# First projections of a two-layer trunk: x loaded with features as rows, scaled after the products

## The chip, the cores and the metric

The kernel runs on one core of one Trainium2 chip. The time is device time in microseconds, the median of three runs; the profile is one more execution, recorded by the hardware profiler. PE (TensorE) multiplies matrices, DVE (VectorE), ACT (ScalarE) and POOL (GpSimd) work elementwise, SP (SyncE) and ACT issue DMA transfers. PSUM is the memory that PE writes its products into, in eight banks here of 128 x 512 floats.

## The reference

The input x has 512 rows (tokens) of 1024 features, in float32. Two layers follow one another; only the start of the first is touched here:

```python
h = rms_norm(x, ev_pre_g)                 # x * rsqrt(mean(x*x) + 1e-6) * g, by row
c_q, c_kv, k_rope, dq, dk, dv = split_cols(h @ w_in, (256, 128, 32, 512, 512, 512))
q = heads_first(rms_norm(c_q, cq_g) @ w_uq, 8)        # latent attention (MLA)
kv = heads_first(rms_norm(c_kv, ckv_g) @ w_ukv, 8)
o_mla = mla_attention(q_nope, q_rope, k_nope, rope(k_rope, pos), v_mla)
o_diff = diff_attention(...)              # on dq, dk, dv: softmax 1 - lambda * softmax 2
x = x + rms_norm(concat(o_mla, o_diff) @ w_out, ev_post_g)
x = x + rms_norm(conv_ffn(rms_norm(x, ffn_pre_g), ...), ffn_post_g)
```

The row factor rsqrt(mean(x*x) + eps) can be taken out of a product with w_in, since it belongs to a row of x and the product sums over features; the weight g cannot, since it belongs to a feature. Where a second norm follows (c_q, c_kv), the row factor cancels but for eps: the norm of the unscaled product with eps * (mean(x*x) + eps) in place of eps is the same number. The second layer (dilated and stick-breaking attention) and its FFN follow in the same manner and are not touched.

## The kernel before, in words

Every float32 product is made of three products of a shorter format: `mm3` multiplies the high half by the high half, high by low and low by high. So every operand is split: ACT rounds it to its high half (`wh`, `xh`), DVE subtracts to get the low half (`wl`, `xl`). For weights the class `Weights` does this: `load` issues one DMA on SP's queue into one of three raw buffers `wraw`, `split` makes the halves in one of five pairs of buffers, `next` hands out a pair and keeps `depth` units ahead. A raw buffer comes free when its low half is made, and SP issues its transfers in order.

The opening, in `trunk` and `even`, goes as follows. SP loads X3, the last 128 tokens of x, then the norm weights, the identity for transposes, the four units of `ev_w_c` (416 columns of w_in, two feature blocks of 128 in a unit) and the other tiles X2, X1, X0. Meanwhile PE multiplies zeros (`warm`, 16 products). For each tile in the order 3, 2, 1, 0, `normalise` takes the square sum on ACT (`mean_square`), the power on POOL (`rstd`), scales X by row and by weight on DVE into `xn`, and `turned` transposes `xn` in eight blocks of 128 x 128 on PE; `split` then makes `xh` and `xl`, with features as rows. Products follow: for each tile 24 products of 416 columns into a bank `ac`, then the norms of c_q and c_kv by square sums of `ac` and the rotary part `ra`, all into `ctok`, four transposes into `tc`, and the split into `omh`/`oml`. Then `diff_qk` makes dq and dk of head 0 (48 products `aqk` of 512 columns), and 72 products `auq`, `auk`, `auv` make the queries `mq`, keys `mk` and values `mv` of the latent attention. `tables` loads the masks and slopes on ACT's queue and computes lambda. All this is put in order by the framework's scheduler.

The attention loop after it is written out by hand (`manual_schedule`): for each of 32 units a score product `sps`, a softmax on DVE and ACT, transposes `tpp`, and between them `Fill`, which hands out single products of `diff_v` (values of the differential attention) and of `diff_qk` for heads 1 to 3, so that PE has work while it waits. dq leaves PSUM through ACT with its scale, dk through DVE, dv through both by turns. PSUM banks have tags: three `a`, two `s`, and one each of `t`, `o`, `n`.

The host function `layout` only cuts and permutes the arrays.

Of the kernel before, what the change touches and what calls it, by code (L numbers as in the profile page):

```python
# [9 lines left out]
F32 = mybir.dt.float32  # L10
# [7 lines left out]
P = 128  # L18
S = 512
# [9 lines left out]
WARM = 16  # L29
# [57 lines left out]
def trunk(tc, A, out):  # L87
# [3 lines left out]
    with ExitStack() as top:  # L91
# [39 lines left out]
        load_x(3)  # L131

# [14 lines left out]
        units += [(A["ev_w_c"][u], 832) for u in range(4)]  # L147
# [26 lines left out]
        def rstd(ms, more=None):  # L174
# [3 lines left out]
            POOL.tensor_tensor(v[:, :n], ms, epst[:, :n], ALU.add)  # L178
# [5 lines left out]
        def mean_square(src):  # L184
# [4 lines left out]
            return rstd(ms[:])  # L189
# [383 lines left out]
        def even():  # L573
            with ExitStack() as es:
# [6 lines left out]
                g_pre = gain("ev_pre_g", 0)  # L581
                nc.sync.dma_start(ident[:], A["ident"])
                for n, i in enumerate(ORDER[1:]):
                    W.load()
                    load_x(i)
# [24 lines left out]
                def diff_qk(h, z):  # L610
# [5 lines left out]
                    if z == 0:  # L616
                        ACT.activation(dq[h], acc, AF.Copy, scale=-0.125)
                    else:
                        DVE.tensor_copy(dk[h], acc)

                def diff_v(tiles):
# [9 lines left out]
                    DVE.tensor_copy(dv[:, tiles[0]], accs[0])  # L631
                    ACT.copy(dv[:, tiles[1]], accs[1])
# [34 lines left out]
                def tables():  # L667
# [8 lines left out]
                    nc.scalar.dma_start(lamb, A["ev_lam"].partition_broadcast(P))  # L676
                    v = chp.tile([P, 8], F32, tag="lam", name="lam", bufs=1)
# [42 lines left out]
                with ExitStack() as e1:  # L720
# [4 lines left out]
                    for n, i in enumerate(ORDER):  # L725
                        normalise(i, g_pre, xnT, "tn" if i % 2 else "ss")()
                        W.ahead((2, 3, 4, 4)[n])

                    with ExitStack() as e2:
# [5 lines left out]
                        wc = [W.next() for _ in range(4)]  # L735
                        nc.sync.dma_start(cgain[:, :256], A["ev_cq_g"][0:1, :].partition_broadcast(P))
                        nc.sync.dma_start(cgain[:, 256:], A["ev_ckv_g"][0:1, :].partition_broadcast(P))
                        nc.sync.dma_start(rtab[:], A["rope_tok"])
                        nc.sync.dma_start(qtab[:], A["rope_q"])
                        for i in ORDER:  # L740
                            t = slice(i * P, (i + 1) * P)
                            a = bank("a", "ac")
# [20 lines left out]
                            for k in range(4):  # L763
                                PE.transpose(tp[:, k], ctok[:, k], ident[:])
# [752 lines left out]
```

## Time and profile before

| what | us |
|---|---|
| median of three runs | 1161.83 (1159.96 to 1161.96) |
| the profiled execution | 1159.68 |
| its span | 1157.9 |
| PE, DVE, ACT, POOL busy | 1139.7, 813.0, 555.1, 61.8 |
| first warm-up product | 1.05 |
| first transposes of x | 8.10 |
| first product of the projections | 11.22 |
| first score product of the attention loop | 62.89 |

The span runs from the first to the last instruction of the profiled execution. Line numbers (L263) are lines of the kernel; a helper's line stands for all who call it, so `L263` to `L265` are the three products of `mm3`. PE is counted as busy from the start of a product to its modelled end, and products overlap; their cadence is read from start to start. The granted clock of PE is 0.998 on average.

### The profile page before, as it was taken

The numbers are of one execution on the slowest core, as the hardware profiler recorded it, in microseconds if no ns is written. First come the engines' busy times: TensorE is split into PE (matmuls) and PEld (weight loads), VectorE is DVE, ScalarE is ACT, GpSimd is POOL, SyncE is SP. The second block draws the span as 40 slices with busy tenths as digits, with TensorE's granted clock in tenths as the row PEclk, the third lists the DMA queues.
The fourth block names the chain that finished last, engine by engine and source line by source line (L and its number), as shares of the span: only waits on it lengthen the run. The fifth ranks groups of instructions, "written<-read, shape, count | busy, mean of one in ns | idle before, by whom it ended". The sixth has DMA issues, their size and how long they took to land.

```text
span 1157.9 us, 15198 instructions
## 1 busy us (share of the span) xinstructions
PE 1139.7 (98%) x5668; PEld 936.2 (81%) x5668; DVE 813.0 (70%) x1431; ACT 555.1 (48%) x940; POOL 61.8 (5%) x139
## 2 busy tenths in 40 slices
PE   8999999999999999999999999999999999999997
PEld 7876677898888888888778877888988888888886
DVE  6676677558667667899873565576676766779897
ACT  5555555345444434456543454554443443445562
POOL 2100022210000000000020000002000000000002
PEclk9999999999999999999999999999999999999999
DMA  8410122243332332355634212222232323324461
GB/s 304 149 55 1 55 92 68 79 149 110 95 106 91 92 109 73 109 159 170 226 119 150 73 61 94 90 67 94 93 110 96 105 91 95 105 82 138 146 207 74
DMA packets 39195, 126.82 MB, mean 110 GB/s; under 512 B 4689, under 2 KB 6353, under 8 KB 39121
## 3 DMA queue, kind: packets, MB, share of 16 engines
q1 hardware_dynamic: 37056, 122.11, 32.5%
q10 hardware_dynamic: 2064, 3.74, 1.0%
q8 instruction: 45, 0.74, 0.3%
q14 instruction: 30, 0.24, 0.1%
HBM read 117.95 MB, written 6.29 MB: 107 GB/s over the span
## 4 chain that ended last, share of the span: by engine, by line
PE 45%; issue 2%; DVE 1%; POOL 1%; ACT 1%; POOLq 0%; DVEq 0%; ACTq 0%
PE u L264 7%; PE u L265 7%; PE u L263 7%; PE acc L263 3%; PE acc L264 3%; PE acc L265 3%; PE apt L263 3%; PE apt L264 3%; PE apt L265 3%; PE cp L1182 1%; PE apv L263 1%; PE apv L265 1%; PE apv L264 1%; PE o L1266 1%; PE o L1343 1%
## 5 line engine op out<-in xcount | busy, mean ns | idle before, releaser
L73 DVE TENSOR_TENSOR wl<-wraw,wh 128x1024 fp32r<-128x1024 f32 (+1 forms) x189 | 228.8, 1218 | 179.0 <-ACT wh L72 178.6
L72 ACT CAST wh<-wraw 128x1024 fp32r<-128x1024 f32 (+1 forms) x189 | 195.8, 1046 | 273.1 <-PE u L264 179.7
L264 PE MATMUL u<-xl,wh 128*128 128x512 f32 (+1 forms) x768 | 285.3, 372 | 0.1
L265 PE MATMUL u<-xh,wl 128*128 128x512 f32 (+1 forms) x768 | 285.2, 372 | 0.0
L263 PE MATMUL u<-xh,wh 128*128 128x512 f32 (+1 forms) x768 | 284.9, 372 | 0.1
L264 PEld LDWEIGHTS u<-xl,wh 128*128 128x128 f32 x768 | 144.6, 188 | 25.4 <-DVE xl L172 0.3
L265 PEld LDWEIGHTS u<-xh,wl 128*128 128x128 f32 x768 | 144.6, 188 | 25.1
L263 PEld LDWEIGHTS u<-xh,wh 128*128 128x128 f32 x768 | 144.4, 188 | 25.2 <-ACT xh L171 0.6
L264 PE MATMUL acc<-wl,gh 128*128 128x512 f32 (+1 forms) x250 | 96.9, 387 | 0.0
L265 PE MATMUL acc<-wh,gl 128*128 128x512 f32 (+1 forms) x250 | 96.9, 387 | 0.0
L263 PE MATMUL acc<-wh,gh 128*128 128x512 f32 (+1 forms) x250 | 96.8, 388 | 0.0
L417 ACT ACTIVATE y<-y 128x512 f32<-128x512 f32 x44 | 27.7, 632 | 84.9 <-DVE y L415 84.9
L412 ACT ACTIVATE y<-u,cw 128x512 f32<-128x512 f32 x88 | 67.2, 771 | 1.8 <-PE u L265 1.8
L415 DVE SCALAR_TENSOR_TENSOR y<-u,cw,y 128x510 f32<-128x510 f32 x88 | 65.6, 747 | 2.5
L413 DVE SCALAR_TENSOR_TENSOR y<-u,cw,y 128x511 f32<-128x511 f32 x88 | 65.1, 744 | 0.9 <-ACT y L412 0.9
L178 POOL TENSOR_TENSOR rv<-ms,epst 128x1 f32<-128x1 f32 x39 | 10.9, 283 | 921.7 <-ACT junk L230 843.5
L263 PEld LDWEIGHTS acc<-wh,gh 128*128 128x128 f32 x250 | 46.9, 188 | 10.2 <-issue 0.5
L596 ACT ACTIVATE s<-s,st 128x128 f32<-128x128 f32 (+3 forms) x64 | 35.8, 560 | 40.1 <-DVE st L594 23.2
L265 PEld LDWEIGHTS acc<-wh,gl 128*128 128x128 f32 x250 | 46.9, 188 | 9.6
L264 PEld LDWEIGHTS acc<-wl,gh 128*128 128x128 f32 x250 | 47.0, 188 | 9.5
L263 PE MATMUL apt<-xh,wh 128*128 128x512 f32 x128 | 50.6, 396 | 0.0
L264 PE MATMUL apt<-xl,wh 128*128 128x512 f32 x128 | 50.0, 391 | 0.0
(315 smaller groups left out, 1956.9 us busy)
## 6 DMA issues: line engine op xcount, KB each, us to landing
wraw<-in_ffn_w_up SPq DMA_DIRECT2D x88, 512.0 KB, 3.6
wraw<-in_ffn_w_down SPq DMA_DIRECT2D x44, 512.0 KB, 3.7
wraw<-in_od_w_dqk SPq DMA_DIRECT2D x12, 512.0 KB, 3.6
wraw<-in_ffn_w_down SPq DMA_DIRECT2D x22, 256.0 KB, 2.7
wraw<-in_ev_w_dqk SPq DMA_DIRECT2D x8, 512.0 KB, 3.7
wraw<-in_ev_w_out SPq DMA_DIRECT2D x8, 512.0 KB, 3.4
spill<-X SPq DMA_DIRECT2D x8, 512.0 KB, 2.6
X<-spill SPq DMA_DIRECT2D x8, 512.0 KB, 6.7
```

The lines of the kernel that those rows point to most:

```text
L72: self.nc.scalar.copy(h[:, :w], raw[:, :w])
L73: self.nc.vector.tensor_tensor(l[:, :w], raw[:, :w], h[:, :w].bitcast(F32), ALU.subtract)
L263: PE.matmul(o, lh, rh, start=first, stop=False, skip_group_check=more)
L264: PE.matmul(o, lh, rl, start=False, stop=False, skip_group_check=more)
L265: PE.matmul(o, ll, rh, start=False, stop=last, skip_group_check=more)
L412: ACT.activation(y[:, z], u, AF.Identity, bias=c[:, 3:4], scale=c[:, 2:3])
L413: DVE.scalar_tensor_tensor(y[:, z, 1:], u[:, :S - 1], c[:, 1:2], y[:, z, 1:], ALU.mult, ALU.add)
L415: DVE.scalar_tensor_tensor(y[:, z, 2:], u[:, :S - 2], c[:, 0:1], y[:, z, 2:], ALU.mult, ALU.add)
L417: ACT.activation(y[:, 0], y[:, 0], AF.Silu)
L596: ACT.activation(s[:, :n], s[:, :n], AF.Exp, bias=st[:, 0:1], scale=-1.0, accum_out=st[:, 1:2])
L1182: PE.matmul(zp[:, c + (j2 - j) * P:c + n], tri[:, 0 if j2 == j else 1], part[:, off[j2]:off[j2 + 1]], start=(j2 == j and part is sh), stop ...
L1266: PE.matmul(o12[hp][:, y, r], pt[:, y, rr, g], cv12[:, r, c:c + 64], start=(g == 0), stop=(g == 1))
```

## The change

The host hands over x a second time, with features as rows (`xT`, eight blocks of 128 features by 512 tokens), and the norm weight as columns (`ev_pre_gT`). The blocks are loaded into the buffers `mq`, which are free until the queries are made. `begin_c` rounds xT times the norm weight to `xh` and takes `xl` as the rest, one feature block k at a time, and splits that block's 416 columns of w_c. Nothing is normalised or transposed ahead of the products: x is multiplied without its row factor. The products run for all four tiles together over the first five blocks (`SPREAD`), in four banks, then tile by tile for the last three (`last_c`).

The row factor is made beside them: `square_x` takes the square sums of the tiles X, which are loaded after xT, and POOL makes `rx[0]` (the factor) and `rx[1]` (eps times mean square plus eps). It is put in where products leave PSUM: the norms of c_q and c_kv take `rx[1]` as their eps, the rotary part takes `rx[0]` as a factor, dv is scaled by it on its way out (by DVE and ACT), and dq and dk, whose columns are tokens, are multiplied by `rbc`, the same factor as a row for all partitions. `rbc` comes from four products of a matrix of ones with diagonal matrices and stays in one of the two buffers `gain`. dq now leaves PSUM through DVE in place of ACT.

The stretch is written out by hand under `manual_schedule`, with the transposes of `ctok` and the casts of dq's and dk's weights between the products. `ident`, `rtab` and `cgain` are loaded on ACT's queue in place of SP's. The lambda computation moves from `tables` into a function `lambdas`, called at the fifth unit of the attention loop. The warm-up has 10 products in place of 16.

The diff, each piece moved to the left margin:

```diff
-WARM = 16
+WARM = 10
+SPREAD = 5
...
-load_x(3)
...
-units += [(A["ev_w_c"][u], 832) for u in range(4)]
...
-def rstd(ms, more=None):
+def rstd(ms, more=None, eps=epst):
...
-POOL.tensor_tensor(v[:, :n], ms, epst[:, :n], ALU.add)
+POOL.tensor_tensor(v[:, :n], ms, eps[:, :n], ALU.add)
...
-def mean_square(src):
+def mean_square(src, eps=epst):
...
-return rstd(ms[:])
+return rstd(ms[:], None, eps)
...
-g_pre = gain("ev_pre_g", 0)
-nc.sync.dma_start(ident[:], A["ident"])
-for n, i in enumerate(ORDER[1:]):
-    W.load()
-    load_x(i)
+rx = lead[:, 16:28].rearrange("p (a b) -> p a b", a=3)
+rbc = glob.tile([P, D], F32, tag="gain", name="rbc", bufs=2)[:, :S]
...
-ACT.activation(dq[h], acc, AF.Copy, scale=-0.125)
+DVE.scalar_tensor_tensor(dq[h], acc, -0.125, rbc, ALU.mult, ALU.mult)
...
-DVE.tensor_copy(dk[h], acc)
+DVE.tensor_tensor(dk[h], acc, rbc, ALU.mult)
...
-DVE.tensor_copy(dv[:, tiles[0]], accs[0])
-ACT.copy(dv[:, tiles[1]], accs[1])
+DVE.tensor_scalar(dv[:, tiles[0]], accs[0], rx[:, 0, tiles[0]:tiles[0] + 1], None, ALU.mult)
+ACT.activation(dv[:, tiles[1]], accs[1], AF.Copy, scale=rx[:, 0, tiles[1]:tiles[1] + 1])
...
+    return g, lamb, lj
+def lambdas(g, lamb, lj):
...
-for n, i in enumerate(ORDER):
-    normalise(i, g_pre, xnT, "tn" if i % 2 else "ss")()
-    W.ahead((2, 3, 4, 4)[n])
+gcol = lead[:, 8:16]
+nc.scalar.dma_start(gcol, A["ev_pre_gT"])
+raws, wc, acs = {}, [], [bank(tag, "ac") for tag in "aaao"]
+def fetch(k):
+    nc.sync.dma_start(mq[k][:], A["xT"][k])
+    if k % 2 == 0:
+        raws[k // 2] = wpool.tile([P, 1024], F32, tag="wraw", name="wraw", bufs=3)
+    c = slice((k % 2) * 416, (k % 2 + 1) * 416)
+    (nc.scalar if k == 0 else nc.sync).dma_start(raws[k // 2][:, c], A["ev_w_c"][k // 2, :, c])
+def begin_c(k):
+    if k % 2 == 0:
+        wc.append(W.pair())
+    h, l = wc[k // 2]
+    c = slice((k % 2) * 416, (k % 2 + 1) * 416)
+    raw = raws[k // 2][:, c]
+    ACT.activation(xh[:, k], mq[k][:], AF.Copy, scale=gcol[:, k:k + 1])
+    ACT.copy(h[:, c], raw)
+    DVE.scalar_tensor_tensor(xl[:, k], mq[k][:], gcol[:, k:k + 1], xh[:, k].bitcast(F32),
+                             ALU.mult, ALU.subtract)
+    DVE.tensor_tensor(l[:, c], raw, h[:, c].bitcast(F32), ALU.subtract)
+def product_c(i, k):
+    t = slice(i * P, (i + 1) * P)
+    h, l = wc[k // 2]
+    c = slice((k % 2) * 416, (k % 2 + 1) * 416)
+    mm3(acs[3 - i][:, :416], xh[:, k, t], xl[:, k, t], h[:, c], l[:, c], k == 0, k == KD - 1)
+def square_x(i):
+    junk = chp.tile([P, D], BF16, tag="junk", name="junk", bufs=1)
+    r = [rx[:, n, i:i + 1] for n in range(3)]
+    ACT.activation(junk[:], X[i][:], AF.Square, scale=D ** -0.5, accum_out=r[2])
+    POOL.tensor_tensor(r[1], r[2], epst[:, :1], ALU.add)
+    POOL.tensor_tensor(r[0], r[1], mhalf[:, :1], ALU.pow)
+    POOL.tensor_tensor(r[1], r[1], epst[:, :1], ALU.mult)
...
-wc = [W.next() for _ in range(4)]
-nc.sync.dma_start(cgain[:, :256], A["ev_cq_g"][0:1, :].partition_broadcast(P))
-nc.sync.dma_start(cgain[:, 256:], A["ev_ckv_g"][0:1, :].partition_broadcast(P))
-nc.sync.dma_start(rtab[:], A["rope_tok"])
-nc.sync.dma_start(qtab[:], A["rope_q"])
-for i in ORDER:
-    t = slice(i * P, (i + 1) * P)
-    a = bank("a", "ac")
-    for k in range(KD):
-        wh, wl = wc[k // 2]
-        c = slice((k % 2) * 416, (k % 2 + 1) * 416)
-        mm3(a[:, :416], xh[:, k, t], xl[:, k, t], wh[:, c], wl[:, c], k == 0, k == KD - 1)
-    rq = mean_square(a[:, 0:256])
-    rk = mean_square(a[:, 256:384])
+ctoks = {}
+def squares_c(i):
+    a = acs[3 - i]
+    e = rx[:, 1, i:i + 1]
+    ctoks[i] = mean_square(a[:, 0:256], e), mean_square(a[:, 256:384], e)
+def norm_c(i):
+    a = acs[3 - i]
+    rq, rk = ctoks[i]
+    r = rx[:, 0, i:i + 1]
...
-DVE.tensor_tensor(ra[:, 0], a[:, 384:416], rtab[:, i, 0], ALU.mult)
-DVE.tensor_tensor(ra[:, 1, 0:16], a[:, 400:416], rtab[:, i, 1, 0:16], ALU.mult)
-DVE.tensor_tensor(ra[:, 1, 16:32], a[:, 384:400], rtab[:, i, 1, 16:32], ALU.mult)
+for o, c, z, d in ((ra[:, 0], 384, 0, 0), (ra[:, 1, 0:16], 400, 1, 0),
+                   (ra[:, 1, 16:32], 384, 1, 16)):
+    n = o.shape[1]
+    DVE.scalar_tensor_tensor(o, a[:, c:c + n], r, rtab[:, i, z, d:d + n],
+                             ALU.mult, ALU.mult)
...
+    ctoks[i] = ctok
+def turn_c(i):
...
-    PE.transpose(tp[:, k], ctok[:, k], ident[:])
+    PE.transpose(tp[:, k], ctoks[i][:, k], ident[:])
+t = slice(i * P, (i + 1) * P)
...
-for z in range(2):
-    Fill(diff_qk(0, z)).end()
-tables()
+W.depth = 1
+ones = dv[:, 2, :P]
+POOL.memset(ones, 1.0)
+for k in range(KD):
+    fetch(k)
+for i in ORDER:
+    load_x(i)
+for _ in range(2):
+    W.load()
+nc.sync.dma_start(qtab[:], A["rope_q"])
+W.load()
+with tc.manual_schedule(engines=everything):
+    for k in range(KD):
+        begin_c(k)
+        if k == 1:
+            nc.scalar.dma_start(ident[:], A["ident"])
+            nc.scalar.dma_start(rtab[:], A["rope_tok"])
+        if k == 3:
+            nc.scalar.dma_start(cgain[:, :256], A["ev_cq_g"][0:1, :].partition_broadcast(P))
+            nc.scalar.dma_start(cgain[:, 256:], A["ev_ckv_g"][0:1, :].partition_broadcast(P))
+        if k < SPREAD:
+            for i in ORDER:
+                product_c(i, k)
+    square_x(3)
+    square_x(2)
+    def last_c(i):
+        for k in range(SPREAD, KD):
+            product_c(i, k)
+    last_c(3)
+    squares_c(3)
+    square_x(1)
+    norm_c(3)
+    last_c(2)
+    squares_c(2)
+    square_x(0)
+    norm_c(2)
+    last_c(1)
+    begun = cast(W)
+    squares_c(1)
+    rest(*begun)
+    turn_c(3)
+    last_c(0)
+    norm_c(1)
+    squares_c(0)
+    turn_c(2)
+    dq0, dk0 = [Fill(diff_qk(0, z)) for z in range(2)]
+    dq0(8)
+    norm_c(0)
+    begun = cast(W)
+    dq0(4)
+    turn_c(1)
+    rest(*begun)
+    dq0(6)
+    turn_c(0)
+    dq0(5)
+    dk0(12)
+    rows = bank("s", "rows", NT, P)
+    for i in ORDER:
+        d = dv[:, 3, i * P:(i + 1) * P]
+        DVE.tensor_scalar(d, ident[:], rx[:, 0, i:i + 1], None, ALU.mult)
+        PE.matmul(rows[:, i], ones, d, start=True, stop=True)
+    ACT.copy(rbc, rows.rearrange("p a b -> p (a b)"))
+    dk0(11)
+    dq0.end()
+    dk0.end()
+W.depth = 5
+small = tables()
...
-assert len(W.made) == 13
-made = {9: 14, 27: 15, 30: 16}
+assert len(W.made) == 9
+made = {9: 10, 27: 11, 30: 12}
...
+if n == 4:
+    lambdas(*small)
...
-r = {"x": a["x"][0]}
+r = {"x": a["x"][0], "xT": a["x"][0].T.reshape(KD, P, S), "ev_pre_gT": a["ev_pre_g"][0].reshape(KD, P).T}
```

## The prediction, made before the run

> **What bounds the kernel now.** I read the page first, then busy time by stage.
>
> ```profile
> span 1157.9 us, 15198 instructions
> ...
> 0.00:62.89 62.89, 59.00 (x297) 51.35 (x297) 39.31 (x79) 35.27 (x70) 10.67 (x32) 1.00 0.58 208
> ...
> 62.89:165.00 102.11, 101.60 (x517) 69.85 (x515) 71.69 (x252) 54.28 (x158) 6.50 (x12) 1.00 0.15 47
> ```
>
> A row of stages gives start:end, length, then busy time of PE, weight loads, DVE, ACT and POOL, clock, DMA share, GB/s. The attention stage from 62.89 us has PE busy 101.6 of 102.1 us. The opening loses 3.9 us outright, and fills more with warm-up products. So the opening was read next, in order of time.
>
> ```profile
> 0.74 0.38 SPq L129 DMA_DIRECT2D X<-in_x  x1
> ...
> 1.05 6.64 PE L137 MATMUL warm<-zero 128*128 128x128 f32 x32 [1.05 <-DVE zero L134]
> ...
> 5.14 1.06 ACT L188 ACTIVATE junk<-X 128x1024 bf16<-128x1024 f32 x1 [2.67 <-DMA X<-in_x]
> ...
> 11.22 0.46 PE L263 MATMUL ac<-wh,xh 128*128 128x416 f32 x1 [1.80 <-ACT xh L171]
> ...
> 13.04 0.46 PE L265 MATMUL ac<-wh,xl 128*128 128x416 f32 x1
> ...
> 62.89 0.61 PE L807 MATMUL sps<-mk,mq 128*128 128x128 f32 x4
> ...
> PE ac L263 <- ACT xh L171: 1.8, 1, 1.8
> ...
> PE sps L807 <- DVE st L594: 0.5, 1, 0.5
> ```
>
> A row gives start, length, engine, line, output and inputs. The first product of the projections starts at 11.22 us: ahead of it stand X3's load (landed 5.14), its square sum, the normalisation, the transposes and the split. Its third partner waits until 13.04. The last two rows are from the list of waits: PE waits 1.8 us for the first `xh`, and once 0.5 us later on in the first 110 us. So what bounds the kernel is TensorE's queue of products behind a late start, and a microsecond off the opening is a microsecond off the end if the attention stage still begins without a new wait.
>
> **The change part by part.** The cadence of PE's work, from neighbouring starts:
>
> ```profile
> 15.25 0.35 PE L264 MATMUL ac<-wl,xh 128*128 128x416 f32 x1
> ...
> 15.44 0.60 PE L211 MATMUL tp<-ident,xn 128*128 128x128 f32 x4
> ...
> 15.79 0.43 PE L265 MATMUL ac<-wh,xl 128*128 128x416 f32 x1
> ...
> 17.20 0.35 PE L265 MATMUL ac<-wh,xl 128*128 128x416 f32 x1
> ...
> 17.39 0.35 PE L263 MATMUL ac<-wh,xh 128*128 128x416 f32 x1
> ...
> 39.76 0.39 PE L604 MATMUL aqk<-xh,wh 128*128 128x512 f32 x1
> ...
> 39.99 0.39 PE L606 MATMUL aqk<-xl,wh 128*128 128x512 f32 x1
> ...
> 63.25 0.48 PE L604 MATMUL av<-wh,xh 128*128 128x512 f32 x1
> ```
>
> A 416-column product costs 0.19 us (17.20 to 17.39), a 512-column one 0.227 (39.76 to 39.99). Four transposes between two products make 0.54 us of 0.19 (15.25 to 15.79), so 0.35, and with the longer next one 0.4. A plain 128x128 product costs 0.18 (62.89 to 63.25 holds two).
>
> Before, check of the method: start 11.22, 96 products of 0.19 (18.2), 48 for dq0/dk0 and 72 for auq/auk/auv of 0.227 (27.2), six groups of x transposes and four of c (10 x 0.4 = 4.0) give 60.6; the other 2.3 us to 62.89 are the early waits. After: the eight x groups are gone, four `rows` products come (0.7), so PE has 18.2 + 27.2 + 1.6 + 0.7 = 47.7 us of work behind its start.
>
> *The start.* Now it hangs on k = 0: 256 KB of xT and 208 KB of w_c.
>
> ```profile
> wraw<-in_ffn_w_down SPq DMA_DIRECT2D x22, 256.0 KB, 2.7
> ...
> wraw<-in_ffn_w_down SPq DMA_DIRECT2D x44, 512.0 KB, 3.7
> ...
> 10.00:11.00 1.00, 0.00 (x0) 0.00 (x0) 0.23 (x1) 1.00 (x3) 0.19 (x1) 1.00 1.03 421
> ...
> L201 DVE SCALAR_TENSOR_TENSOR xn<-X,rr,gain 128x512 f32<-128x512 f32 x8 | 5.8, 747 | 7.7 <-POOL rr L181 7.7
> ...
> L73 DVE TENSOR_TENSOR wl<-wraw,wh 128x832 fp32r<-128x832 f32 x4 | 4.1, 1019 | 0.5 <-ACT wh L72 0.5
> ...
> L73 DVE TENSOR_TENSOR wl<-wraw,wh 128x1024 fp32r<-128x1024 f32 x1 | 1.2, 1219 | 0.0
> ...
> L72 ACT CAST wh<-wraw 128x832 fp32r<-128x832 f32 x4 | 3.5, 887 | 2.0 <-DMA wraw<-in_ev_w_c 2.0
> ...
> L72 ACT CAST wh<-wraw 128x1024 fp32r<-128x1024 f32 x1 | 1.1, 1059 | 0.0
> ...
> 1.19 1.28 ACT L188 ACT_TABLE_LOAD   x1 [1.19 <-PEq L1509]
> ```
>
> The rows are DMA issues (us to landing last), a window (GB/s last), groups (mean ns of one before the second bar). A load of 256 KB alone lands 2.7 us after its issue, so 3.4; X3 with twice the bytes landed 4.4 after its own, at 5.14. I take 4.4 us, since alibi, the gain column and the next tiles fly beside it. The activation table load (1.28) now stands behind the gain column's landing and ends by then if that lands by 3.1. From the 832 and 1024 widths a cast is 0.83 ns and a subtraction 1.04 ns a column: ACT 0.63 for 512, 0.54 for 416; DVE 0.59 for 416, and 0.75 for the scaled `xl` (L201's kind). The second product needs `wl`: 4.4 + 0.63 + 0.75 + 0.59 = 6.4 us, my effective start (bounds: 5.4 with the lone load, 7.2 with X3's landing).
>
> *Feeding k = 1 to 7.* PE needs 12 x 0.19 = 2.3 us for a k of all four tiles; ACT 1.2, DVE 1.35, and 0.47 MB at 421 GB/s 1.1 us. So SPREAD = 5 rows cover the loads, and the four DMA issues (`ident`, `rtab`, two `cgain`) that move into ACT's order there, 0.38 us each like X3's on SP; each also waits for an earlier landing, of alibi, xT or `ident`, which comes before the next xT tile that ACT would wait for anyway. The eight normalisations (0.75 each) and the eight splits of transposes that go free DVE and ACT for this. Work ends without a stall at 6.4 + 47.7 = 54.1.
>
> *The waits that come.* ACT now squares X three to four tiles deep among the square sums of `ac`.
>
> ```profile
> L188 ACT ACTIVATE junk<-X 128x1024 bf16<-128x1024 f32 x3 | 3.2, 1059 | 0.4 <-DMA X<-in_x 0.4
> ...
> 24.60 0.38 ACT L188 ACTIVATE junk<-ac 128x256 bf16<-128x256 f32 x1 [0.55 <-PE ac L265]
> ...
> 25.41 0.56 POOL L181 TENSOR_TENSOR rr<-rv,mhalf 128x1 f32<-128x1 f32 x1
> ...
> 41.57 0.23 DVE L679 CUSTOM_DVE_ANT_0 small<-small 128x64 f32<-128x64 f32 x1 [1.24 <-DMA small<-in_ev_lam]
> ...
> 42.99 0.14 DVE L683 TENSOR_SCALAR lam<-lam 128x1 f32<-128x1 f32 x1
> ...
> 46.76 0.69 DVE L619 COPY dqk<-aqk 128x512 f32<-128x512 f32 x1 [0.74 <-PE aqk L608]
> ...
> 43.17 0.59 ACT L617 ACTIVATE dqk<-aqk 128x512 f32<-128x512 f32 x1
> ```
>
> PE finishes tile 3 at 6.4 + 69 x 0.19 = 19.5. Behind it in ACT's order stand three pairs of square sums (about 1.0 each with their reads), X1 and X0 (1.06 + 0.19 each) and the cast of dq's weights (1.06), whose low half (1.22 on DVE) the third dq0 product needs. That cast follows two pairs and both X: 19.7 + 2.0 + 2.5 + 1.06 = 25.3, low half 26.6; PE arrives at 25.4 and loses some 0.6. Tile 1's norm: its pair ends at 26.3, POOL 27.1 (0.2 and 0.56), DVE with low half, a split and six small instructions 29.2, against PE at 29.1 after twelve dq0 products. Tile 0's pair stands behind a split and two copies on ACT and ends near 29.2, its norm near 31.8, against PE at 31.0. Together 0.9. One auq product has been placed ahead of most of dk0 and needs tile 0's `omh`, which ACT makes near 34.7 behind the casts of dk and uq (1.06 each) and copies; PE asks at 33.9: 0.8. At the end of dk0, near 41 us, DVE still owes weight subtractions and key copies; dq0 and dk0 are evicted late, then two more subtractions of 1.22 stand ahead of the first `mq` eviction (0.69), while three banks serve: PE waits 0.8 for the bank of the second auq, 1.8 for that of auv. Sum of waits 4.9 (bounds 0, if those queues drain a little sooner, and 8, with each chain half as long again). Attention begins at 59.0 instead of 62.9: 3.9 earlier.
>
> *Costs in the attention stage.* Three dq evictions move from ACT (0.59) to DVE (about 0.7), and seven small lambda instructions come in at the fifth unit, about 1.3 us with the wait for ACT's Exp (41.57 to 43.13 before, with other work between): 3.4 us more on DVE, which is idle 30 of 102 us there while PE has no slack. I take 0.5; bounds 0 and 3.4. Row scales on `dv` and `dk` ride in evictions that existed: nothing.
>
> *At nothing.* ffn_pre_g now waits for the buffer that the row scales hold and is issued behind the w_out loads:
>
> ```profile
> 141.46 43.35 SPq L50 DMA_DIRECT2D wraw<-in_ev_w_out  x8
> ...
> L962 DVE SCALAR_TENSOR_TENSOR t<-X,rr,gain x8: 739/744/768, 217.9 to 244.4; 128x512 f32<-128x512 f32 x8
> ```
>
> These end near 185 us, its first use is at 217.9. Without that cover it would cost its landing, 3.7 us like the other 512 KB loads.
>
> *Sum.* 3.9 - 0.5 = 3.4 us. The profiled execution took 1159.68 (span plus 1.8), so 1156.3; the median of the runs shown stands 2.15 above it, so 1158.4.
>
> **The warm-up.** It shrinks from 16 to 10 products.
>
> ```profile
> L137 PEld LDWEIGHTS warm<-zero 128*128 128x128 f32 x10 | 2.2, 329 | 1.0 <-DVE zero L134 1.0
> ...
> L137 PEld LDWEIGHTS warm<-zero 128*128 128x128 f32 x10 | 1.8, 272 | 0.0
> ...
> L265 PEld LDWEIGHTS ac<-wh,xl 128*128 128x128 f32 x16 | 3.0, 188 | 0.2 <-DVE xl L172 0.2
> ```
>
> The first row is from 1 to 3 us, the second from 6 to 7.7 us, the third from 8 to 24. A warm-up weight load took 329 ns at first, 272 on average at the end, 188 afterwards: PE ran slow until about 7 us, though the granted clock reads 1.00. Ten warm-ups at 6.64 / 16 end at 5.2, then PE idles for 0.7 to 1.2 us, and the speed-up may not have come when products begin. If the gap starts the count anew at 6 us, products run for another 6 us at 188/329 of their speed: 2.6 us lost, of which later waits on ACT and DVE give some back. I take 2.0 for that case, bounds 0 and 2.6, and 0 for the forecast, since the gap is a sixth of the busy time before it.
> [...]
>
> **The rivals.**
> *The waits don't form* (0.14). For it: they are chains of sub-microsecond rows with 0.2 us to spare here and there. Time 1158.4 - 4 = 1154.4.
> *A slow clock at the start* (0.16), as above: 1160.4, within the resolution. Against it: the gap is short beside the busy time.
> *Slower: ACT held by X* (0.13). ACT works in order and squares X1 and X0 ahead of dq's cast, and X now loads behind xT and w_c. Ahead of X0's end stand 2.1 MB of xT, 1.7 of w_c, 2.1 of X, 1.3 of alibi and mask, 0.4 of small tables: 7.6 MB, at 421 GB/s from 3 us done at 21.1; ACT asks at 22 to 23. Each microsecond past that moves dq0 and two norms one to one. From a landing at 28 (300 GB/s on the way) the kernel is slower. For it: 2 KB and smaller rows in place of 4 KB ones, and loads that wait for earlier landings. Against: 421 GB/s where no buffer held the loads. Time 1158.4 + 6 = 1164.4.
> *Nothing comes through* (0.05): DVE's added 3.4 us in the attention stage fall wholly on PE: 1161.3.
>
> **How the numbers follow.** The forecast holds 0.52 (own range 1156.5 to 1159.4); with the first rival faster by over 0.2% has 0.66 (0.2%, or 2.3 us, is about what this kernel's runs can tell from no change). Within 0.2%: slow clock and nothing, 0.21. Slower 0.13. The range for 8 in 10 runs from 1153.5, just under the first rival, to 1162.5, which leaves the slower case and a little of each end out.
>
> **What would show it.** Right: no transposes of xn; the first `ac` product near 5.7 and steady cadence from 6.5; the end of the last `ac` product near 25; the first score product near 59; waits on DVE near 41 to 47 us; attention length within a microsecond of 102. Wrong: a first product after 8 us (loads or table load), ACT idle on X1 or X0, `ac` products 0.35 us apart (clock), or a longer attention stage with PE waiting for DVE.

## The result and the profile after

Beside each other on one chip the kernel before took 1161.45 us (median of 8 runs, 1159.51 to 1161.96) and the changed kernel 1157.8 us (8 runs, 1155.01 to 1159.1): a ratio of 0.9971, 95% interval 0.9959 to 0.9982, or 3.65 us. The profiled execution took 1156.68 us against 1159.68 before, 3.00 us less. Repeated on another chip, the changed kernel gave 1157.35 us against 1161.28, ratio 0.9970 (0.9959 to 0.9981).

The stages of the changed kernel (start:end, length, busy time of PE, weight loads, DVE, ACT and POOL, clock, DMA share, GB/s), cut where the first score product starts and 102.09 us later:

```profile
span 1154.9 us, 15146 instructions
...
0.00:59.91 59.91, 55.04 (x260) 46.80 (x261) 36.62 (x73) 36.30 (x73) 10.42 (x37) 1.00 0.68 236
59.91:162.00 102.09, 101.62 (x516) 69.76 (x514) 73.23 (x260) 53.27 (x155) 7.29 (x12) 1.00 0.15 47
```

The score products start at 59.91 us in place of 62.89: 2.98 us earlier, and the span is 3.0 us shorter. So the gain lies in the opening. In the 102 us behind it PE is as busy as before (101.62 us against 101.60), and a score product of the differential attention that came at 158.28 us now comes at 155.56, 2.72 earlier: the attention stage gives back 0.3, although DVE does 73.23 us in it in place of 71.69.

How the opening runs now, from the timelines of PE, ACT and DVE (start, length, engine, line, operation, then the idle time before it and what ended it):

```profile
3.66 1.28 ACT L741 ACT_TABLE_LOAD   x1 [3.66 <-DMA mq<-in_xT]
4.95 0.72 ACT L741 ACTIVATE xh<-mq,lead 128x512 fp32r<-128x512 f32 x1
5.58 0.52 ACT L742 CAST wh<-wraw 128x416 fp32r<-128x416 f32 x1
...
6.16 0.45 PE L261 MATMUL ac<-wh,xh 128*128 128x416 f32 x1 [0.47 <-ACT wh L742]
7.02 0.46 PE L262 MATMUL ac<-wl,xh 128*128 128x416 f32 x1 [0.41 <-DVE wl L745]
7.31 0.35 PE L263 MATMUL ac<-wh,xl 128*128 128x416 f32 x1
...
19.05 1.06 ACT L756 ACTIVATE junk<-X 128x1024 bf16<-128x1024 f32 x1 [1.14 <-DMA X<-in_x]
...
20.41 1.06 ACT L756 ACTIVATE junk<-X 128x1024 bf16<-128x1024 f32 x1 [0.20 <-DMA X<-in_x]
...
21.59 0.38 ACT L186 ACTIVATE junk<-ac 128x256 bf16<-128x256 f32 x1
...
23.14 0.34 PE L263 MATMUL ac<-wh,xl 128*128 128x416 f32 x1
24.07 0.44 PE L798 MATMUL tc<-ident,ctok 128*128 128x128 f32 x2 [0.59 <-DVE ctok L789]
24.72 0.44 PE L798 MATMUL tc<-ident,ctok 128*128 128x128 f32 x2 [0.21 <-DVE ctok L791]
...
26.50 0.34 PE L263 MATMUL ac<-wh,xl 128*128 128x416 f32 x1
26.73 0.44 PE L798 MATMUL tc<-ident,ctok 128*128 128x128 f32 x2
27.38 0.44 PE L798 MATMUL tc<-ident,ctok 128*128 128x128 f32 x2 [0.22 <-DVE ctok L791]
28.51 0.50 PE L603 MATMUL aqk<-xh,wl 128*128 128x512 f32 x1 [0.22 <-DVE wl L653]
...
44.57 1.05 ACT L73 CAST wh<-wraw 128x1024 fp32r<-128x1024 f32 x1 [1.97 <-DMA wraw<-in_ev_w_dv]
...
46.11 0.58 ACT L893 COPY mk<-auk 64x512 f32<-64x512 f32 x1
...
45.65 1.23 DVE L74 TENSOR_TENSOR wl<-wraw,wh 128x1024 fp32r<-128x1024 f32 x1 [0.97 <-ACT wh L73]
46.80 1.28 DVE L884 TENSOR_TENSOR mq<-auq,qtab 128x512 f32<-128x512 f32 x2
...
46.74 0.50 PE L261 MATMUL auv<-wh,omh 128*128 128x512 f32 x1 [1.40 <-ACT mk L893]
```

And two rows from the list of PE's waits in the first 110 us (line, releaser, us in total, times, longest):

```profile
PE tc L798 <- DVE ctok L789: 0.6, 1, 0.6
...
PE auq L261 <- ACT omh L169: 0.3, 1, 0.3
```

The reader is to see four things. The first product comes at 6.16 us in place of 11.22, the second at 7.02, and from 7.31 to 23.14 PE keeps its cadence of 0.19 us without a wait. Then tile 3's four transposes, which could follow at 23.33, are done only when the next product starts at 24.91: about 1.2 us are lost, because ACT got X3 at 19.05 and X2 at 20.41 and came to the square sums of tile 3 only at 21.59. Tile 2's transposes lose another 0.5. The last loss is at `auv`, 1.4 us: PE waits for ACT's copies of the keys out of a bank of `auk`, and the second of them begins only at 46.11, since ACT first casts the weights of dv, which it gets at 44.57. DVE is held by the same weights: it takes their low half ahead of the `mq` evictions, which start at 46.80, after `auv` has begun.

### The profile page after: what moved, and what is told of

The parts are those of the page before. It is cut to its first block, busy times and chain, and to the rows that moved or that the text cites. A ratio compares the mean times of both kernels' runs of the same rounds, so it can differ in the third digit from the quotient of the medians.

```text
span 1154.9 us, 15146 instructions
## 1 busy us (share of the span) xinstructions
PE 1136.1 (98%) x5632; PEld 931.7 (81%) x5632; DVE 812.9 (70%) x1435; ACT 555.4 (48%) x941; POOL 63.4 (5%) x144
## 4 chain that ended last, share of the span: by engine, by line
PE 45%; issue 2%; DVE 1%; POOL 1%; ACT 1%; POOLq 0%; DVEq 0%; ACTq 0%
PE u L262 7%; PE u L263 7%; PE u L261 7%; PE acc L261 3%; PE acc L263 3%; PE acc L262 3%; PE apt L261 3%; PE apt L262 3%; PE apt L263 3%; PE cp L1287 1%; PE apv L261 1%; PE apv L263 1%; PE apv L262 1%; PE o L1371 1%; PE o L1448 1%
## 5 line engine op out<-in xcount | busy, mean ns | idle before, releaser
L74 DVE TENSOR_TENSOR wl<-wraw,wh 128x1024 fp32r<-128x1024 f32 x183 | 222.2, 1222 | 178.4 <-ACT wh L73 178.1
L73 ACT CAST wh<-wraw 128x1024 fp32r<-128x1024 f32 x183 | 190.2, 1050 | 271.4 <-PE u L262 179.4
L176 POOL TENSOR_TENSOR rv<-ms,epst 128x1 f32<-128x1 f32 x27 | 7.6, 285 | 894.5 <-ACT junk L228 843.3
```

Of the source, the lines that this page charges most:

```text
L73: self.nc.scalar.copy(h[:, :w], raw[:, :w])
L74: self.nc.vector.tensor_tensor(l[:, :w], raw[:, :w], h[:, :w].bitcast(F32), ALU.subtract)
```

## The experiments

A place in the profile tells the opening apart better than a total does (runs of one kernel differ by 3 to 4 us, and the last section says what goes with it). As markers I use the first score product and the first product of the feed-forward layer, which was at 234.43 us before and at 231.74 after.

| kernel | median us (runs) | ratio to before, 95% | first ac | first score product | first feed-forward product |
|---|---|---|---|---|---|
| before | 1161.45 (8) | | 11.22 | 62.89 | 234.43 |
| changed | 1157.8 (8) | 0.9971 (0.9959 to 0.9982) | 6.16 | 59.91 | 231.74 |
| e10_after, the same again | 1157.35 (7) | 0.9970 (0.9959 to 0.9981) | 6.25 | 60.57 | 232.52 |
| e1_warm16 | 1156.23 (4) | 0.9954 (0.9939 to 0.9969) | 6.82 | 60.75 | 232.57 |
| e2_warm2 | 1159.84 (10) | 0.9975 (0.9959 to 0.9991) | 6.23 | 61.78 | 233.58 |
| e3_spread0 | 1163.81 (10) | 1.0023 (1.0012 to 1.0033) | 6.75 | 65.06 | 236.91 |
| e4_sched | 1157.67 (10) | 0.9971 (0.9960 to 0.9981) | 6.20 | 60.33 | 232.23 |
| e5_late | 1158.83 (12) | 0.9978 (0.9968 to 0.9989) | 6.16 | 61.40 | 233.26 |
| e6_staged | 1155.12 (5) | 0.9946 (0.9935 to 0.9958) | 6.18 | moved (below) | 229.60 |
| e7_both | 1154.91 (5) | 0.9943 (0.9930 to 0.9956) | 6.22 | 56.40 | 228.32 |
| e11_both, the same again | 1155.34 (5) | 0.9955 (0.9943 to 0.9968) | 6.18 | 58.67 | 230.54 |
| e8_xpose | 1171.32 (4) | 1.0085 (1.0072 to 1.0098) | 14.84 | 73.80 | 245.66 |
| e9_const | 1161.49 (10) | 1.0003 (0.9994 to 1.0012) | 10.54 | 65.04 | 236.61 |

**The warm-up.** Two kernels change one number of the changed kernel.

```
-WARM = 10
+WARM = 16        (e1_warm16)
+WARM = 2         (e2_warm2)
```

> One part undone: 16 warm-up products, as before the change, in place of 10. The first product of the projections then stands behind the last warm-up, near 8.0 us in place of 6.16, so the second product's wait for wl (0.4 us) goes and the steady stretch begins 1.0 to 1.2 us later. Theory (tile 3's and tile 2's norms hang on X's loads, not on PE): most of that is taken back, since PE now idles 1.2 us for tile 3's norm and 0.5 us for tile 2's; the first score product comes at 59.9 to 60.4 us and the total is 0 to 0.5 us above the changed kernel's. Rival (a microsecond at the start is a microsecond at the end): the first score product at 61.0 us, the total 1.1 us above.

The first product came at 6.82, not 8.0, and the second followed at once, at 7.09: the steady stretch begins where it began with ten. So both theories lack their premise, a start 1.0 to 1.2 us later. The score products came 0.84 us later, from longer waits at tile 3 (0.9 for 0.6; X3's square sum began at 19.42) and at `auv` (1.9 for 1.4), both places that hang on loads; the median came out lower, and its interval overlaps that of the changed kernel. The six products that the change took away cost or saved nothing that these runs can tell.

> 2 warm-up products in place of 10, so PE is idle from about 2 us until the first product of the projections near 6.2 us. It asks whether TensorE's speed depends on what stood before. [...] Rival (the speed does not hang on the warm-up): 0.19 us apart from the first on, first score product 59.9 us, total as the changed kernel.

With two warm-ups the timeline of PE shows another cadence at the start:

```profile
6.23 0.72 PE L261 MATMUL ac<-wh,xh 128*128 128x416 f32 x1 [3.95 <-ACT wh L742]
7.09 0.72 PE L262 MATMUL ac<-wl,xh 128*128 128x416 f32 x1
7.60 0.55 PE L263 MATMUL ac<-wh,xl 128*128 128x416 f32 x1
7.95 0.55 PE L261 MATMUL ac<-wh,xh 128*128 128x416 f32 x1
...
10.37 0.41 PE L262 MATMUL ac<-wl,xh 128*128 128x416 f32 x1
10.62 0.35 PE L263 MATMUL ac<-wh,xl 128*128 128x416 f32 x1
```

The products are 0.35 us apart (7.60 to 7.95) until 10.37, the next two 0.25 (10.37 to 10.62), and behind that the cadence of 0.19 is back. So the speed does hang on the warm-up, and the rival falls: with ten warm-ups, over at 5.69, PE was at full speed from its first product at 6.16, which took 0.45 us (0.72 with two), although it had just idled 0.47 us; with two, and 4 us of idle time, it was slow to 10.4. That is 4.1 us from its first product (6.23 to 10.37), and what ended the slow stretch there no run shows. The granted clock of the profile reads 1.00 through all of this start. The loss at the start (some 1.5 us: the eleventh product begins at 10.37 in place of 8.82) was hidden in part behind the norms of tiles 3 and 2, whose waits are gone here; a second loss came at `auv`, as in e5 below.

**The order of the products.**

```
-SPREAD = 5
+SPREAD = 0       (e3_spread0: tile by tile from the start)
```

> One part undone: the products go tile by tile from the start (tile 3 over all eight k first) in place of five rows of k over all four tiles. Theory: tile 3 uses a k every 0.57 us while ACT and DVE need 1.2 to 1.35 us to make one, so the products wait for the split until k = 7 at about 6.8 + 7 x 1.35 = 16.3 us or, with the loads, 18.5 us; behind it stand three tiles of 4.6 us each: last ac product near 31 to 32 us in place of 26, with less idle behind it: tile 3's norm then hides behind tile 2's products. First score product 62 to 64 us, total 2 to 4 us above the changed kernel's (1160 to 1162, about the time before). Rival (the order of the products does not matter because the norms' loads set the pace): first score product within 0.7 us of 59.9.

The place (65.06) and the total went past the theory's own range: slower than the changed kernel by some 6 us (0.0052 by the ratios), and slower than the kernel before. The last `ac` product came at 33.27 (expected 31 to 32). What the theory had left out stands in the stages (clock in the third column from the end):

```profile
8.00:18.00 10.00, 8.33 (x19) 4.65 (x18) 7.26 (x13) 6.38 (x12) 0.00 (x0) 0.50 0.89 318
18.00:34.00 16.00, 15.80 (x85) 15.03 (x85) 7.08 (x21) 9.46 (x26) 8.55 (x24) 0.99 0.81 315
```

From 8 to 18 us PE waits on and off for the split, and its clock is granted at half: 19 products in 10 us. Rows of k over all four tiles, part of this change, are worth more than the whole gain: 5.2 us at the first score product, the halved clock included.

**The written order.**

```
-                        with tc.manual_schedule(engines=everything):
+                        with ExitStack():          (e4_sched)
```

> One part undone: the opening stretch's order is left to the scheduler in place of the written one; all else is as changed. Theory: the written order is worth little by itself, since TensorE's work is the same and the chain X load, square, norm sets the same waits: first score product 59.5 to 61 us, total within 1 us of the changed kernel's. Rival (the written order carries the gain): the scheduler's order puts transposes or evictions ahead of work that is ready, first score product beyond 62 us, total 2 us or more above.

As the theory had it: score products at 60.33, median 1157.67. The written order carries no part of the gain that can be measured.

**The loads of alibi and mask.** They are taken out of `tables()`, which is called near the start, and issued after dk's products.

```
+                def biases():
+                    for n in range(2):
+                        alibi.append(...)
+                        nc.scalar.dma_start(alibi[n][:], A["alibi"][:, 2 * n:2 * n + 2])
+                    nc.scalar.dma_start(dv[:, 0], A["mla_mask"])
...
+                            biases()          (behind dk's products; e5_late)
```

> The loads of alibi (two of 512 KB) and of the mask are issued after dk's products in place of near the start; nothing else moves. Theory (tile 3's norm is late because X's tiles land late, 1.14 us behind ACT's asking for X3, and X shares the DMA engines with alibi): X3 and X2 land 1.3 to 2 us earlier, the idle time of 1.2 us ahead of tile 3's transposes and 0.5 us ahead of tile 2's shrink to 0.6 us or less together, the first score product comes at 58.3 to 59.2 us in place of 59.9, the total 0.7 to 1.6 us lower. Rival (ACT's own queue of square sums makes the norm late, X only seems to): ACT waits less for X, but the square sums of ac end where they did, the two waits keep 1.4 us or more, and the total is the same.

The first half of the theory held: X3's square sum began at 17.80 in place of 19.05, the wait of 0.6 us for tile 3 is gone, and the last `ac` product came at 25.29 in place of 26.50. (Without this edit that square sum began between 18.20 and 20.00 in the executions of the changed kernel, e1, e2 and e6; with it, here and below, between 17.44 and 18.79.) Yet the score products came 1.5 us later. From the timelines of e5, PE and then ACT:

```profile
43.51 0.39 PE L263 MATMUL auk<-omh,wl 128*128 128x512 f32 x1
46.74 0.80 PE L261 MATMUL auv<-wh,omh 128*128 128x512 f32 x1 [2.85 <-ACT mk L896]
...
43.29 1.05 ACT L73 CAST wh<-wraw 128x1024 fp32r<-128x1024 f32 x1 [3.95 <-DMA wraw<-in_ev_w_dv]
```

The loads now stand before dv's weights, which ACT awaits 3.95 us; PE waits 2.85 at `auv` in place of 1.40. Then its clock halves, in e5 (the stages of the first fence) as in e2 (the second):

```profile
45.00:47.00 2.00, 0.26 (x1) 0.26 (x2) 1.94 (x3) 1.68 (x3) 0.00 (x0) 0.94 0.87 260
47.00:49.00 2.00, 2.00 (x5) 1.58 (x6) 1.08 (x2) 0.57 (x1) 0.00 (x0) 0.50 0.78 266
49.00:51.00 2.00, 2.00 (x8) 1.60 (x7) 0.30 (x1) 0.02 (x1) 0.00 (x0) 0.70 0.61 227
```

```profile
47.00:49.00 2.00, 1.94 (x6) 1.52 (x7) 0.93 (x3) 0.58 (x1) 0.00 (x0) 0.76 0.86 258
49.00:51.00 2.00, 2.00 (x6) 1.60 (x5) 0.48 (x1) 0.00 (x0) 0.00 (x0) 0.50 0.33 129
51.00:53.00 2.00, 2.00 (x9) 1.58 (x9) 0.79 (x2) 0.00 (x0) 0.00 (x0) 0.89 0.00 0
```

The half clock lasts 0.24 + 2.0 + 1.2 = 3.4 us in e5 (time at 0.50 that makes the means) and by that would cost 1.7. The 1.7 is half of those 3.4 us, an estimate. `auv` begins at 46.74 in both kernels, so the longer wait takes back all that was won before it, and the 1.5 us by which the score products come later are what the slow clock cost here.

**The weights fetched less far ahead.**

```
-                        W.depth = 5
+                        W.depth = 1
...
+                            W.ahead((5, 6, 7, 9)[p2])        (in the loop over p2; e6_staged)
```

> The weights of the two-map projections are fetched and split four places less far ahead, so that DVE evicts the first mq ahead of the split of dv's weights. Theory (the bank of auv is late because DVE takes the low half of dv's weights, itself late behind a load, ahead of that eviction): PE's wait of 1.4 us at auv goes, the first score product comes at 58.4 to 58.9 us, the total 1 to 1.5 us lower. Rival (attention absorbs it: what DVE did not do early it owes in the attention stage, where it has added work already): the first score product is earlier but the attention stage lengthens from 102.1 to 103 us or more, and the total is within 0.5 us.

The wait at `auv` is gone from the list of waits: DVE evicts the first `mq` at 43.00, and `auv` starts at 44.72, ahead of ACT's key copies (45.20), for which it had waited in the changed kernel. The scheduler put the first two score products early here (45.84 us), so that place can't be compared; the feed-forward layer begins 2.14 us earlier, more than the 1.4 us of that wait, since tile 3's wait of 0.6 us did not come in this execution either. The median is 1155.12, and the interval of its ratio lies below that of the changed kernel. The rival, that attention takes it back, falls.

**Both edits.**

> The two edits together: alibi and mask loaded later, and the weights fetched less far ahead. Theory (two separate waits, each on the path): the gains add, 1.7 to 3 us; the first score product at 57.0 to 58.2 us, total 1155 to 1156 where the changed kernel has 1157.8. Rival (the queue ahead of auv takes back what the start gains): no better than the second edit alone, first score product 58.4 to 58.9 us.

In e7 the score products come at 56.40 and the feed-forward layer begins 3.42 us earlier than in the changed kernel; alone, the loads' edit had lost 1.5. What it lacked was a DVE that evicts `mq` first: dv's weights land late here too (ACT waits 2.83 us for them, and its key copies come at 44.00), but `mq` is evicted from 42.56 on and `auv` starts at 43.35 without a wait.

> The two edits together (alibi and mask loaded later, weights fetched less far ahead), once more, beside the changed kernel on the same chip. Theory: the first score product again near 56.4 us, 3.5 us ahead of the changed kernel's, and the median 2.5 to 4 us under that of the changed kernel in this call. Rival (half clock in later stretches gives part of it back each time): 1 to 2 us under.

This execution shows the score products at 58.67, 1.2 us ahead of the changed kernel's and not 3.5. X came later again (X3's square sum at 18.79 in place of 17.44), and tiles 3 and 2 cost about a microsecond; and PE waits 0.7 us at the next `auq` for ACT's key copies, which stand behind dv's weights (ACT waits 3.94 us for these). So something of PE's can hang on them after all. Beside each other the two edits took 1155.34 us and the changed kernel 1157.35, 2.0 us apart, at the upper end of the rival's range; against the kernel before the ratios are 0.9955 (0.9943 to 0.9968) and 0.9970 (0.9959 to 0.9981), and these two intervals overlap. By the totals the second edit alone (1155.12) does as well as both (1154.91 and 1155.34), so what the loads' edit adds to it is not shown, and the rival of e7, no better than the second edit alone, stands.

**What the transposed load is worth.** x is loaded by rows and transposed on TensorE, unnormalised; the rest is as changed.

```
-                        nc.sync.dma_start(mq[k][:], A["xT"][k])
-                        ACT.activation(xh[:, k], mq[k][:], AF.Copy, scale=gcol[:, k:k + 1])
+                        tp = bank("stn"[k % 3], "tx", 4, P)
+                        for i in range(NT):
+                            PE.transpose(tp[:, i], X[i][:, k * P:(k + 1) * P], ident[:])
+                        xk = tp.rearrange("p a b -> p (a b)")
+                        ACT.activation(xh[:, k], xk, AF.Copy, scale=gcol[:, k:k + 1])
```

> One part undone: x with features as rows is not loaded; X is loaded first and TensorE transposes it, 32 transposes as before, unnormalised, straight from the loaded tiles; the norm weight, the row scale and the written order stay as changed. It parts the gain of the transposed load from that of the dropped normalisation. Theory (the transposed load gives most of the gain): transposes of k = 0 need all four X tiles, landed near 6 to 8 us in place of 4.4 for the first xT, and 8 groups of 0.4 us are added to PE: start 2 to 3 us later, work 3.2 us more, waits for the norms gone (X is there early, 1.7 us less): first score product 63 to 65 us, total 3 to 5 us above the changed kernel's (1161 to 1163). Rival (the gain comes from the row scale, which takes the norm off the start): first score product 60 to 61.5 us, total within 1.5 us of the changed kernel's.

Far past both. PE's timeline first, then two stages (clock in the third column from the end):

```profile
12.52 1.97 PE L742 MATMUL tx<-ident,X 128*128 128x128 f32 x8 [6.83 <-DMA X<-in_x]
14.84 0.72 PE L261 MATMUL ac<-wh,xh 128*128 128x416 f32 x1 [0.35 <-ACT wh L745]
```

```profile
6.00:9.00 3.00, 0.00 (x0) 0.00 (x0) 0.00 (x0) 1.28 (x1) 0.00 (x0) 1.00 0.99 382
9.00:20.00 11.00, 6.99 (x23) 5.92 (x24) 2.41 (x4) 2.13 (x4) 0.00 (x0) 0.53 0.78 298
```

All four tiles of x, 2 MB, have to land ahead of the first k, and they land at 12.5, not 6 to 8; PE idles 6.83 us for them, and its clock is at half until 19.7. The start is 8.7 us later, the products to 19.7 at half speed cost 1.8 (eleven, 0.16 us each), and the six groups of transposes behind the first product some 2.4: 12.9 of the 13.9 us by which the feed-forward layer is late. The rest is the balance of waits for the split near 32 us and a shorter wait at tile 3. The edit is no clean undoing, since the kernel before transposes tile by tile and starts on one tile alone. It shows that k over all tiles wants a load that brings a single k, 256 KB in place of 2 MB.

**What the norm off the start is worth.** In the kernel before:

```
-            r = mean_square(X[i][:])
+            r = mean_square(X[i][:]) if xn is not None else mhalf        (e9_const)
```

> The kernel before, with one thing left out: the rows of x are not normalised for the first projections (no square sums of x, a constant column in place of the row scale), so nothing waits for a norm there; the transposes on TensorE, their splits and the order by tiles stay. It leaves out part of the computation and shows what taking the norm off the start is worth by itself. Theory (the norm is only one of the things that the start waits for: the weights landed at 8.28 us and the warm-up ended at 7.69 us before, and the 32 transposes stay): first product at 9.2 to 9.8 us in place of 11.22, first score product 60.9 to 61.9 us in place of 62.89, total 1 to 2 us under the kernel before, so about half of what the change gained or less. Rival (the norm off the start is the gain): first product at 8.7 us or earlier, first score product 60 us or earlier, total 3 us or more under the kernel before.

Neither: no gain at all. The timelines of DVE, ACT and PE in e9, then a stage of it:

```profile
6.96 1.41 DVE L201 SCALAR_TENSOR_TENSOR xn<-X,mhalf,gain 128x512 f32<-128x512 f32 x2 [5.96 <-DMA gain<-in_ev_pre_g]
...
9.60 1.74 ACT L72 CAST wh<-wraw 128x832 fp32r<-128x832 f32 x2
...
7.76 1.32 PE L211 MATMUL tp<-ident,xn 128*128 128x128 f32 x8 [1.47 <-DVE xn L201]
10.54 0.47 PE L263 MATMUL ac<-wh,xh 128*128 128x416 f32 x1 [1.46 <-ACT wh L72]
11.60 0.71 PE L264 MATMUL ac<-wl,xh 128*128 128x416 f32 x1 [0.59 <-DVE wl L73]
```

```profile
12.00:14.00 2.00, 2.00 (x7) 1.90 (x7) 2.00 (x4) 0.89 (x1) 0.00 (x0) 0.50 0.98 369
```

The transposes wait for the gain's load now and the first product for the weights' split, which ACT takes up only behind the split of x, at 9.60, without waiting for a load; the second product is no earlier than before (11.60 against 11.52). Then the clock is at half from about 11 to 17.7 us, which lengthens this execution. But at equal clock the totals agree: at 0.995 five runs of e9 took 1161.5 us on average, and ten of the kernel before, beside them, 1161.9. So the norm alone was not what held the start: the gain's load and the split of the weights stood right behind it.

**The same kernel again.**

> The changed kernel once more, unaltered, beside the next one on the same chip, and a second look at one execution. [...] Median 1156.5 to 1158.5. Rival (the scatter is in the waits themselves): the waits differ by a microsecond between the two looks.

Two waits of this execution of the changed kernel, then stages of the one shown above and of this one:

```profile
PE tc L798 <- DVE ctok L789: 1.4, 1, 1.4
PE auv L261 <- ACT mk L893: 1.3, 1, 1.3
```

```profile
27.00:31.00 4.00, 3.56 (x17) 2.45 (x16) 3.67 (x10) 2.43 (x11) 3.61 (x10) 1.00 0.74 252
...
646.00:650.00 4.00, 3.87 (x17) 3.19 (x18) 3.53 (x9) 1.17 (x1) 0.00 (x0) 1.00 0.54 167
```

```profile
27.00:31.00 4.00, 4.00 (x16) 3.56 (x15) 3.54 (x9) 2.71 (x11) 3.61 (x10) 0.64 0.60 202
...
646.00:650.00 4.00, 3.53 (x11) 2.83 (x12) 3.87 (x9) 0.83 (x1) 0.00 (x0) 0.71 0.60 195
```

The rival has a part: tile 3's wait was 1.4 us in place of 0.6, since X's landing varied (ACT began X3's square sum at 20.00 in place of 19.05). The clock has another: it was at half after that wait (0.64 in the mean from 27 to 31 us) and again from 647.65 us on, behind a wait that the execution shown above has too, 0.82 us long in both, without a halved clock:

```profile
646.47 0.92 PE L1256 MATMUL zp<-sq,sk 64*128 64x256 f32 x4 [0.82 <-DVE z L1260]
```

The odd layer's transposes wait 1.4 us in both, and the clock stays whole behind them.

## Why the prediction was right

It said 1158.4 us (1153.5 to 1162.5) and faster at 0.66; measured 1157.8. Against the profiled execution, its own base, it said 3.4 us and 3.0 came; of the 0.6 us between the medians 0.4 is that base, 1161.83 in three runs and 1161.45 in eight. By its steps:

- *The start, 6.4.* Steady from the second product at 7.02, which makes 6.83: 0.4 late. The load was better than reckoned (xT at 3.66, not 4.4). The mis-sized term is the activation table load: I let it end beside the loads if the gain column landed by 3.1, but that landed near 3.7 (3.0 us after its issue), the table load began with xT's landing at 3.66, and it stood on the path with its 1.28 us (in the kernel before it ran at 1.19, ahead of X's landing; why it waited here no run shows); the scaled copy took 0.72, not 0.63.
- *The work, 47.7, and feeding.* PE kept 0.19 us from 7.31 to 23.14 with no wait, so ACT, DVE and the loads do feed k = 1 to 7. e3 shows that this depends on the rows of k.
- *The waits, 4.9.* 59.91 - 6.83 - 47.7 leaves 5.4 us, of which the places named here make some 4.1, the rest being tenths by which products start slower behind each pause: near in sum, wrong in its parts, so that the sum held is in part luck. Third dq0 product 0.6: 0.4 came (28.51). Tiles 1 and 0, 0.9: nothing came. The early auq product 0.8: about 0.45. The second auq's bank 0.8: 0.1. auv 1.8: 1.4, but released by ACT's key copies and not by DVE's eviction of `mq`, as I had it; both stood behind dv's late weights. In place of the two that did not come stand 1.2 and 0.5 for tiles 3 and 2, which I had given no wait. The step that failed is X's landing: I set ACT's demand for X0 at 22 to 23 us against loads done at 21.1, but ACT asked for X3 already at 17.9 and had it at 19.05. PE, held at tile 3, then came later to the other places, which fits their shorter waits; no run parts that by itself.
- *Attention, 0.5.* From the score products to the feed-forward layer it took 171.54 us before and 171.83 after: 0.3. DVE's added work was hidden but for that at most.
- *At nothing: ffn_pre_g.* From the feed-forward layer's first product to the end of the span: 923.5 before, 923.2 after.
- *Slow clock at the start (0.16).* Did not come with ten warm-ups, came with two: full speed from 10.4 us. In the changed kernel the full speed was there at 6.16, behind an idle stretch of 0.47 us; with two warm-ups the slow stretch was 4.1 us long, not the 6 that I had put on a count begun anew.
- *ACT held by X (0.13).* Its mechanism came, at X3 in place of X0 and at 1.7 us in place of 6.
- *The waits don't form (0.14).* It was not so in the changed kernel. e7 shows what it would be worth: with both edits PE waits little ahead of the score products, and they start at 56.40. The 4 us that I put on this case are near the 3.5 seen there; e11 has 1.2.

The reason behind the forecast, a late start traded for some five microseconds of waits, was right. Which part of the change brings it is less plain. The norm taken off the start gives nothing in the kernel before (e9); without the transposed load the rest of the change loses 13.9 us (e8), and without products over four tiles 5.2 (e3). So the gain needs these together: a transposed load, a k at a time, used over four tiles. How it divides among them can't be told, since each edit brought waits and clocks of its own, and the transposed load was not tried by itself in the kernel before.

## What to carry to other kernels

When a start hangs on a chain, take off the last link in thought and see what stands right behind it: here it was a second load and the split of the weights, and what moved the start was a change that made the first step of everything small (256 KB of xT, 208 KB of weights). A load moved out of one stage's way lands in another's; look at the order on the engines that it would hold up (e5, where that cost all that was won). And an idle stretch of TensorE can cost more than its length: behind 1.4 us (e10), 2.0 (e2) and 2.85 (e5) came 3.4 us at half clock, 1.7 us more by an estimate from half of that, and behind 1.4 and 1.9 us at `auv` (the changed kernel, e1) none.

## What was not expected of the hardware

**Half clock for 3.4 us came behind some short idle stretches.** Half-clock stretches followed idle stretches of 2.85 us (e5), 2.0 (e2) and 1.4 (e10, tile 3), each 3.4 us long; 1.4 us at `auv` in the changed kernel's execution shown first, and 1.9 in e1, were followed by none. So the length of the idle stretch does not settle it.

The stretches at half clock in these executions are one, two or three times 3.41 us long (3.4 in e5; 6.83 in e9, 10.85 to 17.68; 10.24 in e3, 8.06 to 18.30), and the two of e10 begin 621.22 us apart (26.43 and 647.65), 182 times a third of e3's 10.24; why, no run shows. In the 3.41 us ahead of their half clock PE was busy 0.56 us in e5, 1.39 in e2 and 1.79 in e10; in the 3.41 us up to the start of `auv` it was busy 2.01 in the changed kernel (43.33 to 46.74) and 1.54 in e1 (44.16 to 47.57, 3.41 less the idle 1.87), the latter less than e10's 1.79, and no half clock followed. So the busy share does not settle it either. And at `zp` all thirteen executions wait 0.8 us, and in five of them (e2, e7, e8, e9, e10) the clock was at half soon after, in e10 from 647.65 on; at the same place of the changed kernel's execution shown first, with PE busy 2.46 of the 3.41 us up to 647.31, it was not. What decides there stays open.

**The scatter went with the granted clock.** Over the runs of the kernel before that stand beside the experiments, those with a mean clock of 0.994 or 0.995 took 1162.2 us on average (30 runs), those with 0.997 or 0.998 took 1160.2 (21 runs); for e5 it was 1159.9 and 1157.8 (6 runs each). In e2 four runs with 0.998 or 0.999 took 1155.5 to 1156.6 us, and six with 0.995 or 0.996 took 1159.7 to 1162.7. One half-clock stretch of 3.41 us takes 0.0015 off the mean clock, an estimate from its length, 0.50 of the clock and a span of 1155 us, so by that such groups are one to three stretches apart. So two kernels that differ by a microsecond are better compared at a place in the trace ahead of such a stretch, or by runs of equal clock, than by a handful of totals.

**A load's landing moved by a microsecond from one execution to the next.** With the same kernel ACT began X3's square sum at 19.05 and 20.00, and PE waited 0.6 and 1.4 us for tile 3; with both edits that square sum began at 17.44 and 18.79. It is part of the scatter, and my expectations for e6, e7 and e11 had not allowed for it.
